# A hybrid decoder layer on one core: the first FFN's residual transposed by VectorE in 32 x 32 blocks, a pair's fourth difference in place, masks and T1 splits bound anew

## The chip, the cores and the metric

The kernel runs on one core of a Trainium2 chip. The metric is the device time of one execution in microseconds (us), the median over several runs; lower is better. A core has five engines with an instruction stream each: TensorE (PE, matrix products and transposes), VectorE (DVE, elementwise work), ScalarE (ACT, activations and copies), GpSimd (POOL, elementwise work and issuing of DMA) and SyncE (SP, issuing of DMA). Each runs its own instructions in order; semaphores join them. Sixteen DMA engines move data between DRAM and the on-chip memory.

## The reference

One decoder layer over 1024 tokens with 16 learned meta tokens ahead of them (T = 1040 rows, D = 1024), all in float32:

```
h = concat(meta, x)
h = h + 1/2 * swiglu(rms_norm(h, g1), ffn1_w_in, ffn1_w_out)     # D_FF = 2816
u = rms_norm(h, g) @ w_in
o = concat[hgrn2(u), stick_breaking(u)]
h = h + o @ w_out
h = h + 1/2 * swiglu(rms_norm(h, g2), ffn2_w_in, ffn2_w_out)
swiglu(h, wi, wo):  g, u = split(h @ wi);  return (silu(g) * u) @ wo
```

What matters here is the first FFN, `h @ ffn1_w_in`, and the residual `h` that is added behind `ffn1_w_out`. The FFN works on transposed activations (features on the partitions, tokens along the free axis), so the residual is wanted transposed too.

## The kernel before

Float32 products are emulated by pairs: a value is split into a rounded high part and the low rest, and a product takes three matmuls (high-high, low-high, high-low). The FFN products use Strassen's scheme in Winograd's form: the two operands are cut into 2 x 2 blocks, and seven products of block sums replace eight. The seven right-hand operands are B11, B21, B22 and T1 to T4. They are built from the normalised tokens for the way in and from the gated activations for the way out.

**The way in** is `fast_in` (L348 to 577), about 11 to 516 us of the span. It goes over 11 pairs of 128-wide blocks of features; the columns of one pair make two `quad`s (L433), the gate's and then the up projection's. A quad makes seven groups of 12 matmuls of 128x512 (`times`, L424; the matmul is L428) in three banks qa, qb and qc. Its weights are loaded by SP (`block`, L371), combined by POOL (`made`, L377 to 382) and split by ACT and DVE (`operand`, L356 to 361: `wh` L358, `wl` L360). The evictions of the gate's quad go through L499 to 506, those of the up's through L508 to 520; L455 and L460 keep the sums u2 and u3 of one bank that others need (the trace names them `u`). PE's group T3 adds onto the bank qb that u2 is read from, so it waits for that.

**The end of a pair** is `combined` (L522 to 540): from the four gated blocks it makes T1, T2, T3 and T4 and stores them to DRAM (`actD`) for the way out. In this first FFN the subtractions run on DVE (`meta` is given). T1, T2 and T4 are tiles `t` (L530) from a ring of two (`t_bufs`, set with the banks in `run`), so T4 needs T1's tile, that is, T1's store has to be done. T3 is made in place in `sg[0,1]`. In the trace the stores of pair q (0 to 10) of the first FFN are called `act1qT<-t` or `act1qT<-sg` (T1 to T4) and `act1qB<-sg` (B11, B21, B22), so `act14T` belongs to its pair 4 and `act19T` to its pair 9; the texts name pairs and the boundaries behind them by this, act14 to act19. Pairs 0 to 3 are the opened ones, whose quads run interleaved.

**The opening** (`open_tokens`, L735 to 902) runs ahead of and within the first quads. It makes the normalised tokens, T2, T3 (`combine` L821, `second` L837) and later T1, T4 and B22 (`later`, L885) while PE already works on the first pairs. Its order on ACT, DVE and SP is written out by hand in `items` (L867). `halve` (L304) splits one block into high (ACT) and low (DVE). The masks that the attention needs much later are cast from float to bytes by one copy on DVE (L864).

**The residual** is transposed beside the pairs by `turn_x` (L950 to 977): 18 places, 9 row blocks of 128 tokens (the last has 16) times 2 halves of the features. For each place SP loads a row block `xrow` of 128x512, PE transposes its four 128x128 squares into a bank (L966, `xt`), ACT copies them to `xts` (L970) and POOL stores them to DRAM (`xD`, L971). `xrow` and `xts` are single buffers. The way out loads `xD` back as `hT` from about 516 us on (`between` in `run`). Beside it goes `split_ahead` (L142 to 178), which splits weights of the later stages ahead of time: SP loads (L152, `early`), ACT and DVE split (L174, L175, `both`), SP stores (L169).

**Order.** PE's order is written by hand: it is the order of the calls. On the other engines the tile framework's scheduler places the instructions by priorities and what they depend on; `issue_after` adds a bound. `open_ev` starts `turn_x` and the splits as steps; `taken`, called after the evictions, advances them in turn.

Of the kernel before, what the change touches and what calls it, by code (L numbers as in the profile page):

```python
# [11 lines left out]
F32 = mybir.dt.float32  # L12
# [8 lines left out]
P = 128  # L21
# [3 lines left out]
META = 16  # L25
T = META + SEQ
# [14 lines left out]
class Block:  # L41
# [262 lines left out]
    def halve(self, pair, src, j):  # L304

        nc = self.nc
        hi, lo = pair
        nc.scalar.copy(hi[:, j, :], src)  # L308
        nc.vector.tensor_sub(lo[:, j, :], src, hi[:, j, :].bitcast(F32))

    def blocks_a(self, hT, gain, c, n, r, ops):

# [35 lines left out]
    def fast_in(self, ops, n, w_in, actD, openers, ev0, open_ev, feed=None, meta=None, spare=None,  # L348
                between=lambda: None, after_opened=lambda: None, late=lambda: None, taken=lambda at, step=True: None):

        nc = self.nc
# [33 lines left out]
        places = [0]  # L385
# [102 lines left out]
        def pair(f, opened=None):  # L488
            sg = {}
            kept = spare(f // 2) if opened and spare else (None, None, None)  # L490

            def tile_of(i, j):
                pool = ev0 if (i, j) == (0, 0) else ev["p"]
                sg[i, j] = kept[2] if (i, j) == (0, 0) and kept[2] is not None else pool.tile(
                    [P, n], F32, tag=f"sg{i}{j}", name="sg", bufs=2 if (i, j) == (0, 0) else 1
                )
                return sg[i, j]

            def gate(i, j, ps, plus):  # L499
                t = tile_of(i, j)  # L500
                if plus is None:
                    at = nc.scalar.activation(t, ps, AF.Silu)
                else:
                    nc.vector.tensor_add(t, ps, plus)
                    at = nc.scalar.activation(t, t, AF.Silu)
                taken(at)

            def up(i, j, ps, plus):  # L508
                t = sg[i, j]
                if plus is None:  # L510
                    at = nc.vector.tensor_mul(t, ps, t)
                else:
                    u = ev["p"].tile([P, n], F32, tag="u", name="u", bufs=2)
                    nc.vector.tensor_add(u, ps, plus)
                    at = nc.vector.tensor_mul(t, u, t)
                taken(at)
                if (i, j) != (0, 1):
                    nc.gpsimd.dma_start(actD[f // 2, f"B{i + 1}{j + 1}"], t)
                else:
                    combined()  # L520

            def combined():  # L522

                sub = (nc.vector if meta else nc.gpsimd).tensor_sub

                def put(name, t):
                    nc.gpsimd.dma_start(actD[f // 2, name], t)

                def made(x, y):
                    t = ev["p"].tile([P, n], F32, tag="t", name="t", bufs=self.t_bufs)  # L530
                    sub(t, x, y)
                    return t

                t1 = made(sg[0, 1], sg[0, 0])
                put("T1", t1)
                t2 = made(sg[1, 1], t1)
                put("T2", t2)
                sub(sg[0, 1], sg[1, 1], sg[0, 1])
                put("T3", sg[0, 1])
                put("T4", made(sg[1, 0], t2))  # L540

            turned = bool(opened) and not feed
            return [
                quad(f * P, gate, opened, 2 * turned, kept[0]),
                quad(D_FF + f * P, up, opened and "second", 1 * turned, kept[1]),
            ]
# [188 lines left out]
    def open_tokens(self, ops, opened, rows_at, ev, operands):  # L735
# [9 lines left out]
        nc, x = self.nc, self.a["x"][0]  # L745
        stt, sub = nc.vector.scalar_tensor_tensor, nc.vector.tensor_sub
# [15 lines left out]
        def apart(name, pool):  # L762
            return [pool.tile([P, 512], F32, name=f"{name}{j}") for j in range(4)]
# [32 lines left out]
        meta = rp.tile([META, D], F32, name="meta")  # L796
# [40 lines left out]
        def second(j):  # L837
            if j == 0:
                rows_at.close()
                pools["masks"].close()  # L840
                operands("T1", "T3", "T2")
            self.halve(ops["T2"], t2[j], j)
            self.halve(ops["T3"], t3[j], j)

        def roots():
            for i, row in enumerate(rb + [meta]):
# [4 lines left out]
        def scales():  # L851
            for i in (2, 3):
                self.row_scale(rb[i], 4 + i)
            self.row_scale(meta, 8)
# [4 lines left out]
                with self.tc.issue_after(at.ins):  # L859
                    self.masks_cut(sd)  # L860

        def combined(j):
            if j == 1:
                nc.vector.tensor_copy(self.masks, sd)  # L864
# [12 lines left out]
        after = {6: turn_b22, 7: turn_b12, 8: turn_meta}  # L877
        for i in range(2, len(order)):
            if i + 2 < len(order):
                next(order[i + 2])  # L880
            items[i]()
            next(order[i])
            after.get(i, lambda: None)()

        def later():  # L885
            for j in range(4):
                self.halve(ops["T1"], b11[j], j)
            yield
            for j in range(4):
                sub(b21[j], b21[j], t2[j])  # L890
# [12 lines left out]

    def meta_in(self, marks):
# [45 lines left out]
    def turn_x(self, pool, xD):  # L950

        nc = self.nc
        places = [(r0, min(P, T - r0), q) for r0 in range(0, T, P) for q in range(2)]

        def load(i):
            r0, m, q = places[i]
            row = pool.tile([P, 512], F32, tag="xrow", name="xrow", bufs=1)
            self.load_rows(nc.sync, row, r0, m, slice(512 * q, 512 * q + 512))
            return row

        row = load(0)
        yield
        for i, (r0, m, q) in enumerate(places):
            ps = self.pin.tile([P, 4, P], F32, tag="qd", name="xt", bufs=2)
            for k in range(4):
                nc.tensor.transpose(  # L966
                    ps[:, k, :m], row[:m, k * P : (k + 1) * P], self.ident[:m, :m]
                )
            t = pool.tile([P, 4, P], F32, tag="xt", name="xts", bufs=1)
            nc.scalar.copy(t[:, :, :m], ps[:, :, :m])  # L970
            nc.gpsimd.dma_start(  # L971
                xD[4 * q : 4 * q + 4, :, r0 : r0 + m].rearrange("k p t -> p k t"),
                t[:, :, :m],
            )
            if i + 1 < len(places):
                row = load(i + 1)
            yield
# [1247 lines left out]
```

## Time and profile before

| | us |
|---|---|
| time, median of 3 runs (2037.3, 2037.41, 2045.62) | 2037.41 |
| the profiled execution's own time | 2047.66 |
| its span in the profile | 2046.0 |
| PE busy (97% of the span) | 1982.2 |
| DVE busy (66%) | 1350.3 |
| ACT busy (42%) | 869.5 |
| POOL busy (29%) | 595.8 |

The profile is of one execution. A line `L428 PE MATMUL qb<-T,wh ...` names the line of the kernel, the engine, the operation, and out<-in by the program's names. A bracket `[4.90 <-DVE u L460]` behind a row of the timeline is the engine's idle time ahead of it and what ended that. "Granted clock" is the share of full clock pulses that PE was given, 1.00 being full.

### The profile page before, as it was taken

What the parts mean: (1) busy time and instruction counts of PE and PEld (TensorE: products, weight loads), DVE (VectorE), ACT (ScalarE), POOL (GpSimd) and SP (SyncE); (2) the same over time, 40 slices, a digit from 0 to 9 for tenths busy, and PEclk for the clock granted to TensorE, in tenths of its full rate; (3) what the DMA queues carried; (4) which work ended last, traced back from release to release, by engine and by line L of the source; (5) the groups of instructions that cost most, each with busy time, mean ns of one, the idle gap of its engine ahead of it and who ended that gap; (6) DMA issues with size and microseconds to landing.
All of it is one profiled execution on the core that took longest, in us unless ns stands there. A gap on an engine that the chain in (4) does not pass through costs nothing.

```text
span 2046.0 us, 30906 instructions
## 1 busy us (share of the span) xinstructions
PE 1982.2 (97%) x11004; PEld 1660.6 (81%) x11004; DVE 1350.3 (66%) x2036; ACT 869.5 (42%) x1758; POOL 595.8 (29%) x708
## 2 busy tenths in 40 slices
PE   7999989999999999999999998999999999999998
PEld 6778777878788888897988887877888888888887
DVE  7966556777686673326767758549476676666774
ACT  6523333443344544446666644435133333334443
POOL 3453333433000002134333332320354454430000
PEclk9999999999999999999999999999999999999999
DMA  7254667655995514543545256673632332369463
GB/s 210 81 177 157 206 218 225 230 204 196 346 316 163 168 48 159 166 139 107 162 117 142 71 187 201 161 251 140 206 117 94 104 112 94 104 236 308 131 198 137
DMA packets 283099, 347.19 MB, mean 170 GB/s; under 512 B 28017, under 2 KB 183153, under 8 KB 282945
## 3 DMA queue, kind: packets, MB, share of 16 engines
q1 hardware_dynamic: 263376, 287.98, 44.3%
q0 software_dynamic: 18528, 57.23, 7.9%
q8 instruction: 87, 1.43, 0.3%
q14 instruction: 68, 0.55, 0.1%
q10 hardware_dynamic: 1040, 0.00, 0.0%
HBM read 233.75 MB, written 111.38 MB: 169 GB/s over the span
## 4 chain that ended last, share of the span: by engine, by line
PE 82%; DVE 6%; DMA 4%; issue 3%; ACT 2%; POOL 2%; SPq 0%; DVEq 0%; POOLq 0%; ACTq 0%
PE o L679 19%; PE qb L428 16%; PE qc L428 11%; PE qa L428 9%; PE proj L249 5%; PE proj L251 5%; PE proj L250 5%; PE flip L1351 2%; PE wo L249 1%; PE wo L250 1%; PE wo L251 1%; PE mq L935 1%; DMA raw<-in_ffn_w_out_dram 1%; PE lvl L1144 1%; PE oacc L1421 1%
## 5 line engine op out<-in xcount | busy, mean ns | idle before, releaser
L428 PE MATMUL qb<-T,wh 128*128 128x512 f32 x1056 | 352.0, 398 | 20.0 <-DVE u L460 18.0
L428 PEld LDWEIGHTS qb<-T,wh 128*128 128x128 f32 x1056 | 201.9, 191 | 69.4 <-issue 20.3
L428 PE MATMUL qa<-B,wh 128*128 128x512 f32 x696 | 228.5, 393 | 1.8 <-ACT T L308 1.8
L249 PE MATMUL proj<-xh,wh 128*128 128x512 f32 (+2 forms) x640 | 216.5, 338 | 0.8 <-DVE st L1044 0.7
L360 DVE TENSOR_TENSOR wl<-s,wh 128x512 fp32r<-128x512 f32 x160 | 179.3, 1121 | 56.5 <-ACT wh L358 54.4
L679 PE MATMUL o<-t,w 128*128 128x512 f32 x924 | 212.9, 391 | 0.2
L679 PE MATMUL o<-parts 128*128 128x512 f32 x924 | 210.2, 389 | 0.6 <-DVE parts L612 0.6
L251 PE MATMUL proj<-xl,wh 128*128 128x512 f32 (+2 forms) x640 | 209.8, 328 | 0.8 <-DVE xl L1806 0.8
L428 PE MATMUL qb<-T,wl 128*128 128x512 f32 x528 | 209.1, 396 | 0.9 <-DVE wl L360 0.9
L250 PE MATMUL proj<-xh,wl 128*128 128x512 f32 (+2 forms) x640 | 209.8, 328 | 0.0
L358 ACT CAST wh<-s 128x512 fp32r<-128x512 f32 x160 | 99.5, 622 | 246.7 <-PE qb L428 189.2
L679 PEld LDWEIGHTS o<-t,w 128*128 128x128 f32 x924 | 172.6, 188 | 37.8 <-issue 0.8
L679 PEld LDWEIGHTS o<-parts 128*128 128x128 f32 x924 | 173.3, 188 | 36.8 <-DVE parts L612 1.0
L382 POOL TENSOR_TENSOR s<-raw 128x512 f32<-128x512 f32 x80 | 110.5, 1381 | 155.1 <-DMA raw<-in_ffn_w_in_dram 92.3
L428 PEld LDWEIGHTS qa<-B,wh 128*128 128x128 f32 x696 | 130.6, 188 | 29.5 <-ACT T L308 2.2
L428 PE MATMUL qa<-B,wl 128*128 128x512 f32 x348 | 135.5, 389 | 0.0
L358 ACT CAST wh<-raw 128x512 fp32r<-128x512 f32 x120 | 74.5, 621 | 139.2 <-PE qc L428 101.0
L251 PEld LDWEIGHTS proj<-xl,wh 128*128 128x128 f32 x640 | 120.5, 188 | 12.2 <-DVE xl L1806 1.2
L249 PEld LDWEIGHTS proj<-xh,wh 128*128 128x128 f32 x640 | 120.7, 189 | 11.4 <-DVE st L1044 1.2
L250 PEld LDWEIGHTS proj<-xh,wl 128*128 128x128 f32 x640 | 120.6, 188 | 9.1
L1503 POOL TENSOR_TENSOR sig<-sig,keep 128x144 f32<-128x144 f32 (+3 forms) x64 | 81.4, 1273 | 134.0 <-DVE keep L1497 82.5
L428 PEld LDWEIGHTS qb<-T,wl 128*128 128x128 f32 x528 | 101.0, 191 | 22.2 <-DVE wl L360 1.8
(390 smaller groups left out, 4084.1 us busy)
## 6 DMA issues: line engine op xcount, KB each, us to landing
raw<-in_ffn_w_in_dram SPq DMA_DIRECT2D x176, 256.0 KB, 3.5
raw<-in_ffn_w_out_dram SPq DMA_DIRECT2D x121, 256.0 KB, 4.4
w2in<-both SPq DMA_DIRECT2D x28, 512.0 KB, 2.9
raw<-in_w_in_dram SPq DMA_DIRECT2D x25, 512.0 KB, 4.1
ks<-kD SPq DMA_DIRECT2D x32, 260.0 KB, 4.8
wout<-both SPq DMA_DIRECT2D x16, 512.0 KB, 4.1
wh<-w2in SPq DMA_DIRECT2D x27, 256.0 KB, 3.6
wl<-w2in SPq DMA_DIRECT2D x27, 256.0 KB, 3.3
```

Of the source, the lines that this page charges most:

```text
L249: nc.tensor.matmul(ps, wh[:, s], xs, start=k == 0, stop=False)
L250: nc.tensor.matmul(ps, wl[:, s], xs, start=False, stop=False)
L251: nc.tensor.matmul(ps, wh[:, s], xl[:, k, c0 : c0 + n], start=False, stop=k == nk - 1)
L358: nc.scalar.copy(hi, src)
L360: nc.vector.tensor_sub(lo, src, hi.bitcast(F32))
L382: taken(op(t, x, y), False)
L428: nc.tensor.matmul(ps, a[:, k, :], b[:, k, :], start=start and k == 0 and i == 0, stop=k == 3 and i == 2, skip_group_check=True,)
L679: nc.tensor.matmul(banks[bank][m], y[:, m * P : (m + 1) * P], z, start=start and at == 0 and e == 0, stop=q == nq - 1 and e == 2, skip_gro ...
L935: nc.tensor.matmul(ps[at : at + 32, :], self.xm[:, 4 * h + k, :], blocks[i, h][:, k, :], start=h == 0 and kk == 0, stop=h == 1 and kk == 1 ...
L1144: nc.tensor.matmul(ps[:, :, c, :], kp[:, P * c : P * c + P], strided(QA, P * c + n, (512 - n, 2), (2 * n, nb), (1, n)), start=True, stop=True,
L1351: self.nc.tensor.transpose(ps[:m, j, :], src[:, s0 : s0 + m], self.ident)
L1503: nc.gpsimd.tensor_mul(sig, sig, keep[:, 1 : nk + 1])
```

## The change

Three things change, all in the first FFN's way in or beside it.

1. **The residual's transposes.** The rows are cut anew: one place with the 16 meta rows and eight of 128 tokens, times two halves. The two meta places go as before (PE, ACT, POOL). In the other 16, DVE transposes the 128x512 tile in 32x32 blocks (`nc.vector.transpose`), each block in its own place, and four SP stores per place, one for each band of 32 partitions, write each block where the whole transpose has it in `xD`. A store moves 64 KB in runs of 32 elements (128 bytes); before, one POOL store moved the place's 256 KB in runs of 512 bytes.
2. **T4 in place.** With `meta` (the first FFN) T4 is made in `sg[1,0]` and stored from there, not in a third `t`.
3. **Bounds in the opening.** `halve` returns its two instructions; the four T1 splits of `later` are issued after the last T3 split on ACT and DVE. The masks copy is moved from the second `combine` to item 7, behind `keep_b22`.

Taking the changed program's order beside the one before: PE loses the 16 groups of four 128x128 transposes, ACT their 16 copies and POOL their 16 stores. DVE gets 16 transposes; in the pairs act14, act15 and act16 they stand in the stretch between the last split of `both` and `u` (L460), in act17 in the up's quad, and none stands in act18 or act19. T4 stands directly behind T3, ahead of `wl` and of the next pair's `u`. The masks copy goes ahead of the opening's first up-gate addition (L511). SP gets 64 stores, each four behind their transpose, with the next `xrow` load behind them.

```diff
         hi, lo = pair
-        nc.scalar.copy(hi[:, j, :], src)
-        nc.vector.tensor_sub(lo[:, j, :], src, hi[:, j, :].bitcast(F32))
+        return (
+            nc.scalar.copy(hi[:, j, :], src),
+            nc.vector.tensor_sub(lo[:, j, :], src, hi[:, j, :].bitcast(F32)),
+        )
...
                 put("T3", sg[0, 1])
-                put("T4", made(sg[1, 0], t2))
+                if meta:
+                    sub(sg[1, 0], sg[1, 0], t2)
+                    put("T4", sg[1, 0])
+                else:
+                    put("T4", made(sg[1, 0], t2))
...
-            self.halve(ops["T3"], t3[j], j)
+            return self.halve(ops["T3"], t3[j], j)
...
-        def combined(j):
-            if j == 1:
-                nc.vector.tensor_copy(self.masks, sd)
-            combine(j)
...
-            7: keep_b22,
+            7: lambda: (keep_b22(), nc.vector.tensor_copy(self.masks, sd)),
         }
...
-        items.update({8 + j: lambda j=j: combined(j) for j in range(4)})
+        items.update({8 + j: lambda j=j: combine(j) for j in range(4)})
...
-            items[i]()
+            last = items[i]()
...
         def later():
-            for j in range(4):
-                self.halve(ops["T1"], b11[j], j)
+            with self.tc.issue_after(last[0].ins), self.tc.issue_after(last[1].ins):
+                for j in range(4):
+                    self.halve(ops["T1"], b11[j], j)
             yield
...
-        places = [(r0, min(P, T - r0), q) for r0 in range(0, T, P) for q in range(2)]
+        places = [(r0, q) for r0 in [0, *range(META, T, P)] for q in range(2)]
...
-        for i, (r0, m, q) in enumerate(places):
-            ps = self.pin.tile([P, 4, P], F32, tag="qd", name="xt", bufs=2)
-            for k in range(4):
-                nc.tensor.transpose(
-                    ps[:, k, :m], row[:m, k * P : (k + 1) * P], self.ident[:m, :m]
+        for i, (r0, q) in enumerate(places):
+            t = pool.tile([P, 512], F32, tag="xt", name="xts", bufs=1)
+            if r0 == 0:
...
+            else:
+                nc.vector.transpose(t, row)
+                dst = xD.rearrange("k p t -> (k p) t")[512 * q : 512 * q + 512]
+                for b in range(4):
+                    nc.sync.dma_start(
+                        dst[:, r0 + 32 * b : r0 + 32 * b + 32].rearrange("(b d) t -> d b t", d=32),
+                        t[32 * b : 32 * b + 32].rearrange("d (b t) -> d b t", t=32),
+                    )
             if i + 1 < len(places):
                 row = load(i + 1)
             yield
```

More of the change, by code (lines that the diff above doesn't have):

```diff
@@ L952, in turn_x @@
         nc = self.nc
-        places = [(r0, min(P, T - r0), q) for r0 in range(0, T, P) for q in range(2)]
+        places = [(r0, q) for r0 in [0, *range(META, T, P)] for q in range(2)]
         def load(i):
-            r0, m, q = places[i]
+            r0, q = places[i]
             row = pool.tile([P, 512], F32, tag="xrow", name="xrow", bufs=1)
-            self.load_rows(nc.sync, row, r0, m, slice(512 * q, 512 * q + 512))
+            cols = slice(512 * q, 512 * q + 512)
+            if r0 == 0:
+                nc.sync.dma_start(row[:META], self.a["meta_tokens"][:, cols])
+            else:
+                nc.sync.dma_start(row, self.a["x"][0][r0 - META : r0 - META + P, cols])
             return row
@@ L962, in turn_x @@
         yield
-        for i, (r0, m, q) in enumerate(places):
-            ps = self.pin.tile([P, 4, P], F32, tag="qd", name="xt", bufs=2)
-            for k in range(4):
-                nc.tensor.transpose(
-                    ps[:, k, :m], row[:m, k * P : (k + 1) * P], self.ident[:m, :m]
-                )
[L969 to L974, printed above, removed]
+        for i, (r0, q) in enumerate(places):
+            t = pool.tile([P, 512], F32, tag="xt", name="xts", bufs=1)
+            if r0 == 0:
+                ps = self.pin.tile([P, 4, META], F32, tag="qd", name="xt", bufs=2)
+                for k in range(4):
+                    nc.tensor.transpose(
+                        ps[:, k, :], row[:META, k * P : (k + 1) * P], self.ident[:META, :META]
+                    )
+                t = t[:, : 4 * META].rearrange("p (k t) -> p k t", k=4)
+                nc.scalar.copy(t, ps)
+                nc.gpsimd.dma_start(
+                    xD[4 * q : 4 * q + 4, :, :META].rearrange("k p t -> p k t"), t
+                )
+            else:
+                nc.vector.transpose(t, row)
[4 more added lines that the diff above has]
+                        t[32 * b : 32 * b + 32].rearrange("d (b t) -> d b t", t=32),
+                    )
             if i + 1 < len(places):
```

## The prediction

> **What bounds the kernel now.** I read the page first: its engine shares and its costliest groups.
>
> ```profile
> span 2046.0 us, 30906 instructions
> PE 1982.2 (97%) x11004; PEld 1660.6 (81%) x11004; DVE 1350.3 (66%) x2036; ACT 869.5 (42%) x1758; POOL 595.8 (29%) x708
> L428 PE MATMUL qb<-T,wh 128*128 128x512 f32 x1056 | 352.0, 398 | 20.0 <-DVE u L460 18.0
> q1 hardware_dynamic: 263376, 287.98, 44.3%
> ```
>
> PE is busy for 97% of the span, so only two things shorten the kernel: fewer instructions on PE, or less of the 64 us in which PE stands still or runs slowly. The third line says that the first FFN's matmuls (L428) stood still 20.0 us, 18.0 of it for the DVE addition `u` of L460. The view of waits says what is ahead of that addition in DVE (columns: total us, times, longest).
>
> ```profile
> PE qb L428 <- DVE u L460: 18.0, 5, 5.2
> DVE t L531 <- DMA act15T<-t: 5.1, 1, 5.1
> DVE t L531 <- DMA act16T<-t: 4.8, 1, 4.8
> DVE t L531 <- DMA act14T<-t: 3.5, 1, 3.5
> DVE t L531 <- DMA act17T<-t: 3.5, 1, 3.5
> POOL xD L971 <- ACT xts L970: 41.2, 13, 5.1
> ```
>
> At the end of pairs act14 to act17, T4 (the third `t` from a ring of two) waits in DVE until T1's store has landed. The PE timeline shows the first matmul after each of the six pair boundaries that PE feels, with PE's idle time ahead of it in brackets, and the one early stall that the change touches (60.00).
>
> ```profile
> 60.00 0.47 PE L428 MATMUL qa<-B,wh 128*128 128x512 f32 x1 [1.80 <-ACT T L308]
> 249.71 0.77 PE L428 MATMUL qb<-T,wh 128*128 128x512 f32 x1 [4.90 <-DVE u L460]
> 299.64 0.77 PE L428 MATMUL qb<-T,wh 128*128 128x512 f32 x1 [5.23 <-DVE u L460]
> 348.44 0.76 PE L428 MATMUL qb<-T,wh 128*128 128x512 f32 x1 [4.99 <-DVE u L460]
> 398.54 0.50 PE L428 MATMUL qc<-T,wl 128*128 128x512 f32 x1 [0.72 <-DVE wl L360]
> 438.87 0.47 PE L428 MATMUL qb<-T,wh 128*128 128x512 f32 x1 [1.93 <-DVE u L460]
> 483.11 0.47 PE L428 MATMUL qb<-T,wh 128*128 128x512 f32 x1 [0.96 <-DVE u L460]
> ```
>
> The chain of waits (start, duration) gives the wait as one of its links and the groups of 12 matmuls behind the gaps.
>
> ```profile
> 215.27 0.44 PE xt L966 x4
> 218.44 2.72 PE qb L428 x12
> 243.14 5.04 DMA act14T<-t
> 249.71 5.46 PE qb L428 x12
> 299.64 4.68 PE qb L428 x12
> 348.44 5.46 PE qb L428 x12
> 438.87 4.57 PE qb L428 x12
> 483.11 3.00 PE qb L428 x12
> ```
>
> Undisturbed, 12 matmuls take 2.72; after a gap of 4.9 they take 5.46, after one of 1.93 they take 4.57: a second price of the gap, paid at half the granted clock. So a boundary costs its gap plus the excess over 2.72: act14 4.90 + 2.74 = 7.64, act15 5.23 + 1.96 = 7.19, act16 4.99 + 2.74 = 7.73, act17 0.72, act18 1.93 + 1.85 = 3.78, act19 0.96 + 0.28 = 1.24. Together 28.3 us.
>
> **The change, part by part.** *T4 in place.* DVE around the first of these boundaries, and T4 of act18:
>
> ```profile
> 244.08 0.68 DVE L360 TENSOR_TENSOR wl<-s,wh 128x512 fp32r<-128x512 f32 x1
> 248.28 0.69 DVE L531 TENSOR_TENSOR t<-sg,t 128x512 f32<-128x512 f32 x1 [3.51 <-DMA act14T<-t]
> 248.88 0.68 DVE L460 TENSOR_TENSOR u<-qb,p 128x512 f32<-128x512 f32 x1
> 440.15 0.68 DVE L531 TENSOR_TENSOR t<-sg,t 128x512 f32<-128x512 f32 x1
> ```
>
> T4 now overwrites `sg[1,0]`, so it needs that tile's own store (B21) landed, not T1's. The DVE waits 3.51, 5.06 and 4.82 (3.5, 5.1, 4.8 above) leave the path. The order of instructions moves too: T4 now stands directly behind T3. In act14 to 16 it was ahead of `u` already; in act17 to 19 it stood behind (440.15, after PE had its `u` at 438.87) and now puts 0.60 (the pitch 248.28 to 248.88) ahead of `u`.
>
> *Transposes on DVE.* Removed from PE: 16 groups of 4, each 0.44 (215.27): 7.0 us on the engine that sets the end. The two 16-row places keep theirs. Removed elsewhere:
>
> ```profile
> L970 ACT COPY xts<-xt x18: 201/579/582, 100.2 to 455.4; 128x512 f32<-128x512 f32 x16, 128x64 f32<-128x64 f32 x2
> L971 POOL DMA_DIRECT2D xD<-xts x18: 760/770/779, 101.0 to 455.9; - x18
> DMA to landing us min/median/max: 2.7/4.8/6.7
> ```
>
> ACT loses 16 x 0.58 = 9.3 us, POOL 16 x 0.77 = 12.3 and part of the 41.2 of waiting; both are busy under half the span, hidden under PE: 0 on the path. Added to DVE: 16 transposes of 128x512. No row shows that operation. Bounds: from below half of a 128x1024 single-input row, 0.35; from above the dearest copy of that size, the masks' 1.71.
>
> ```profile
> 37.09 1.40 DVE L721 TENSOR_SCALAR row<-row,ss_x 128x1024 f32<-128x1024 f32 x2
> 45.45 0.69 DVE L890 TENSOR_TENSOR b<-b,t 128x512 f32<-128x512 f32 x1
> 49.23 1.71 DVE L864 CAST masks<-sd 128x896 uint8<-128x896 f32 x1
> 59.18 0.68 DVE L511 TENSOR_TENSOR sum<-qa,sum 128x512 f32<-128x512 f32 x1
> ```
>
> I take 0.60, the pitch of the 128x512 additions, which have its shape and type. DVE is 66% busy, so most of the 16 hide in its idle time; in act14, 15 and 16 the new order puts one inside the burst ahead of `u`, where it counts. There PE also arrives 0.44 earlier (its transposes are gone), which widens the gap by as much. The gaps become
>
> - act14: 4.90 - 3.51 + 0.60 + 0.44 = 2.43, long enough to drop the clock (1.93 was): + 1.85 = 4.28
> - act15: 5.23 - 5.06 + 1.04 = 1.21; act16: 4.99 - 4.82 + 1.04 = 1.21; I let neither drop it, since 1.21 is nearer to 0.96 (483.11, followed by 3.00) than to 1.93
> - act17: 0.60 + 0.44 = 1.04 (its `wl` is no longer late; between 0 and this)
> - act18: 1.93 + 0.60 + 0.44 = 2.97, + 1.85 = 4.82
> - act19: 0.96 + 0.60 + 0.28 = 1.84
>
> Sum 14.4; gain 28.3 - 14.4 = 13.9. With the transpose at 0.35, 0.75 more; at 1.71, three times 1.1 and two more clock drops (act15, act16): 7.0 less.
>
> [...]
>
> *Stores.* 16 POOL stores of 256 KB become 64 SP stores of 64 KB, the same bytes in runs of 128 B: 32,768 runs. SP now issues per place four stores and, behind them, the next place's `xrow` load; behind these in SP's queue are the raw weight loads (L371) and the loads and stores of the split-ahead (L152, L169), whose consumers are POOL's and ACT's operand work.
>
> ```profile
> 227.38 2.52 SPq L371 DMA_DIRECT2D raw<-in_ffn_w_in_dram  x4
> 256.00:307.00 51.00, 45.77 (x271) 37.22 (x260) 29.27 (x42) 17.98 (x34) 16.99 (x17) 0.93 0.65 220
> 512.00:563.00 51.00, 50.89 (x297) 40.67 (x296) 32.78 (x55) 19.52 (x35) 3.27 (x6) 1.00 0.97 346
> ```
>
> An issue on SP takes 2.52 / 4 = 0.63, so a place costs SP 2.5 us of every 20.9 (L970: 18 starts from 100.2 to 455.4, 355.2 / 17). On the transfer engines the lower bound is nothing (same bytes); the upper takes q1's mean packet, 0.443 x 16 x 2046 / 263,376 = 55 ns: 32,768 x 55 ns / 16 = 113 us over 355, a share of 0.32 more. In the window 256 to 307 (last columns: granted clock, DMA share, GB/s) that lifts 0.65 to 0.97; and 512 to 563 is a stretch with 0.97 where PE still did 50.89 of 51. So I put 0 on the path, hidden by the depth of the raw buffers; without that cover it is the first rival.
>
> [...]
>
> *Masks and T1 splits.* The masks copy (1.71 at 49.23) leaves the stretch ahead of 59.18, and a subtraction of 0.60 pitch (45.45) or its like comes into it: the 1.80 at 60.00 shrinks to 0.7, a gain of 1.1 (between 0 and 1.8).
>
> **Sum.** 13.9 + 7.0 + 1.1 = 22.0. The profiled execution took 2047.66 (span 2046.0 and 1.66 around it): 2025.7 for it. The timed runs were 2037.41, 2037.3 and 2045.62; they scatter by about one boundary's price (7.2 to 7.7), so the median may have met one fewer late T1. If it met all, 2037.4 - 22.0 = 2015.4; if one fewer (7.4), 2022.8. I take the middle, **2019**.
>
> **Rivals.** *1, slower: DVE waits for the small stores.* `xrow` and `xts` are single buffers, so each DVE transpose waits until the four stores before it have landed and the `xrow` load, itself behind them in SP, too. It decides once issue to landing, now 2.7 to 6.7, comes near the 20.9 between places. Everything behind it in DVE (`u`, `wl`) is then late, at act15's price, 7.2 a place; at half the 16 places 58 us: 2019 + 58 = 2077. For it: 4 times as many runs, SP's queue shared with loads. Against: three times the slowest landing is needed.
>
> *2: the DVE burst is the limit anyway*, T4's wait only covered it. For it: act18 stalls 1.93 with no store in the wait. Against: act15 and 16, where 0.17 remains after the wait. All six boundaries at 4.3 cost 25.8, a gain of 2.5; with 7.0 and 1.1, 10.6: 2026.8.
>
> *3: B21's store takes T1's place.*
>
> ```profile
> 239.52 0.54 POOL L518 DMA_DIRECT2D act14B<-sg  x1 [2.15 <-DVE sg L515]
> ```
>
> Issued at 239.52, it lands at 246.2 if it takes the slowest 6.7; T4, ready at 244.08, waits 2.1. Three times that and two clock drops (3.7): 10.0 less, so 2029. Against: the median landing 4.8 is 244.3, some 0.2 late.
>
> [...]
>
> **Chances.** Forecast 0.57, rival 1 0.14, 2 0.17, 3 0.08, 4 0.04. A measurement here can tell about 0.5%: faster is below 2027.2, slower above 2047.6. The forecast and rival 4 are faster but for 0.03; rival 2 lies on the edge (half and half), rival 3 mostly on the near side of no change: faster 0.68, same 0.18, slower 0.14. The range holds all but rival 1 and the far tail: below, all 28.3 plus 7.0 plus 1.8 gone is 2000, which I don't reach, 2005; above, the dear transpose (2026) and rival 3 with some spread, 2036.
>
> **What would show it.** The waits `DVE t L531 <- DMA act..T` gone; PE's idle time ahead of L428 on `u` L460 from 18.0 to about 10; no PE transposes of 128x128; a DVE transpose row near 0.6; PE gap at 60 us under 1. I am wrong if a wait of DVE's transpose or of `xrow` for a DMA shows with several us a place, if PE's gaps at the boundaries stay near 5, or if raw loads become what L428 waits for.

## The result and the profile after

| | before | after |
|---|---|---|
| time, median of 7 runs (us) | 2040.85 (2037.3 to 2046.82) | 2023.35 (2019.63 to 2031.19) |
| the profiled execution's own time | 2047.66 | 2020.56 |
| PE's first matmul of the way out, from the span's start | 516.35 | 490.57 |

The changed kernel is faster: ratio 0.9915, 95% interval 0.9893 to 0.9937, that is 17.3 us (12.9 to 21.8). The two profiled executions lie 27.1 us apart, because the one of before was 6.8 above its kernel's median and the one of after 2.8 below. The third row is the measure used below: the way in begins with the same first matmul in every run (15.4 to 16.5 us), so the start of the way out tells how long it took. Of the 27.1 us, 25.8 came before that point. One execution of the experiment `bounds_alone` below took 3979.15 us instead of some 2041, for which nothing on record gives a reason; its ratio leaves that one out.

The page of after, the same rows as before:

```profile
span 2018.8 us, 30806 instructions
PE 1964.1 (97%) x10940; PEld 1646.2 (82%) x10940; DVE 1356.4 (67%) x2052; ACT 860.8 (43%) x1742; POOL 583.5 (29%) x692
L430 PE MATMUL qb<-T,wh 128*128 128x512 f32 x1056 | 346.0, 391 | 10.1 <-DVE u L462 7.5
q1 hardware_dynamic: 297136, 292.18, 46.0%
```

PE stood still 7.5 us for `u` instead of 18.0, and its matmuls of that group are at 391 ns instead of 398. The view of waits has no T4 waiting for T1's store any more; what DVE's transposes waited for is this, in the whole run:

```profile
DVE xts L983 <- DMA xD<-xts: 3.4, 1, 3.4
DVE xts L983 <- DMA xrow<-in_x_dram: 1.9, 1, 1.9
```

The view of the tile `xts` gives the operation that the profile before did not have, and the landing of the small stores:

```profile
L983 DVE STREAM_TRANSPOSE xts<-xrow x16: 696/701/712, 117.1 to 355.6; 128x512 f32<-128x512 f32 x16
DMA to landing us min/median/max: 1.9/3.1/6.7
```

The PE timeline at the early stall and the six boundaries (start, duration, idle time ahead of it):

```profile
59.87 0.47 PE L430 MATMUL qa<-B,wh 128*128 128x512 f32 x1 [1.94 <-DVE sum L513]
243.06 0.47 PE L430 MATMUL qb<-T,wh 128*128 128x512 f32 x1 [1.47 <-DVE u L462]
286.22 0.47 PE L430 MATMUL qb<-T,wh 128*128 128x512 f32 x1 [2.05 <-DVE u L462]
328.78 0.47 PE L430 MATMUL qb<-T,wh 128*128 128x512 f32 x1 [1.41 <-DVE u L462]
371.37 0.47 PE L430 MATMUL qb<-T,wh 128*128 128x512 f32 x1 [0.95 <-DVE u L462]
414.16 0.47 PE L430 MATMUL qb<-T,wh 128*128 128x512 f32 x1 [1.65 <-DVE u L462]
457.35 0.47 PE L430 MATMUL qb<-T,wh 128*128 128x512 f32 x1 [1.16 <-ACT both L174]
```

And two of the groups behind these gaps in the chain of waits:

```profile
243.06 2.97 PE qb L430 x12
286.22 3.00 PE qb L430 x12
```

None of the six gaps, 8.7 us in sum, dropped the clock: behind 2.05 the twelve matmuls took 3.00, where behind 1.93 they had taken 4.57 before. The early stall is as long as it was (1.80 before, 1.94 now) and has another releaser.

What is late at the boundaries now shows in DVE's timeline at the third of them. DVE works without a pause from 314.51 to 329, and `u` is the last of a queue:

```profile
314.51 1.60 DVE L362 TENSOR_TENSOR wl<-raw,wh 128x512 fp32r<-128x512 f32 x1
316.03 1.77 DVE L517 TENSOR_TENSOR sg<-u,sg 128x512 f32<-128x512 f32 x1
317.73 1.77 DVE L175 TENSOR_TENSOR both<-early,both 128x512 fp32r<-128x512 f32 x1
319.42 0.68 DVE L516 TENSOR_TENSOR u<-qb,p 128x512 f32<-128x512 f32 x1
...
321.83 0.70 DVE L983 STREAM_TRANSPOSE xts<-xrow 128x512 f32<-128x512 f32 x1
...
326.75 0.68 DVE L543 TENSOR_TENSOR sg<-sg,t 128x512 f32<-128x512 f32 x1
327.35 0.69 DVE L362 TENSOR_TENSOR wl<-s,wh 128x512 fp32r<-128x512 f32 x1
327.95 0.68 DVE L462 TENSOR_TENSOR u<-qb,p 128x512 f32<-128x512 f32 x1
```

The change put the transpose (321.83) into that queue. T4 (326.75) stood ahead of `u` at this boundary before, too, but with its wait of 4.82. Three others take 1.60 to 1.77 instead of 0.68; POOL adds beside them:

```profile
314.28 1.28 POOL L384 TENSOR_TENSOR s<-raw 128x512 f32<-128x512 f32 x1 [5.17 <-DMA raw<-in_ffn_w_in_dram]
315.64 1.62 POOL L384 TENSOR_TENSOR s<-s,raw 128x512 f32<-128x512 f32 x1
317.22 1.73 POOL L384 TENSOR_TENSOR s<-raw 128x512 f32<-128x512 f32 x1
```

So the profile of after raises three questions: which part brought the time, whether T4's wait or its place was the price, and whether POOL's additions make the rest.

### The profile page after: what moved, and what is told of

It reads as the page before. It is cut to its first block, busy times and chain, and to the rows that moved or that the text cites. A ratio compares the mean times of both kernels' runs of the same rounds, so it can differ in the third digit from the quotient of the medians.

```text
span 2018.8 us, 30806 instructions
## 1 busy us (share of the span) xinstructions
PE 1964.1 (97%) x10940; PEld 1646.2 (82%) x10940; DVE 1356.4 (67%) x2052; ACT 860.8 (43%) x1742; POOL 583.5 (29%) x692
## 3 DMA queue, kind: packets, MB, share of 16 engines
q8 instruction: 87, 1.43, 0.3%
## 4 chain that ended last, share of the span: by engine, by line
PE 82%; DVE 7%; DMA 5%; issue 3%; ACT 2%; POOL 1%; SPq 0%; DVEq 0%; POOLq 0%; ACTq 0%
PE o L685 18%; PE qb L430 16%; PE qc L430 11%; PE qa L430 10%; PE proj L249 5%; PE proj L251 5%; PE proj L250 5%; PE flip L1366 2%; DMA raw<-in_ffn_w_out_dram 1%; PE wo L250 1%; PE wo L249 1%; PE wo L251 1%; PE mq L937 1%; PE oacc L1436 1%; PE oacc L1438 1%
## 5 line engine op out<-in xcount | busy, mean ns | idle before, releaser
L430 PE MATMUL qb<-T,wh 128*128 128x512 f32 x1056 | 346.0, 391 | 10.1 <-DVE u L462 7.5
L362 DVE TENSOR_TENSOR wl<-s,wh 128x512 fp32r<-128x512 f32 x160 | 183.4, 1147 | 60.4 <-ACT wh L360 59.3
L430 PE MATMUL qc<-T,wh 128*128 128x512 f32 x352 | 118.6, 398 | 0.0
```

The lines of the kernel that those rows point to most:

```text
L362: nc.vector.tensor_sub(lo, src, hi.bitcast(F32))
L430: nc.tensor.matmul(ps, a[:, k, :], b[:, k, :], start=start and k == 0 and i == 0, stop=k == 3 and i == 2, skip_group_check=True,)
```

## The experiments

The twelve were timed in three sets, each beside the kernel before, and a ratio is to the before of its own set. "Way out" is PE's first matmul of it in the one profiled execution, 516.35 in before and 490.57 in after; before's profiled execution was 6.8 above its kernel's median, so a gain read from this column is larger than the one of the medians.

### One part at a time

`t4_alone` has the second part only:

```diff
-                put("T4", made(sg[1, 0], t2))
+                if meta:
+                    sub(sg[1, 0], sg[1, 0], t2)
+                    put("T4", sg[1, 0])
+                else:
+                    put("T4", made(sg[1, 0], t2))
```

> The kernel before with T4 made in place, nothing else. Theory of the prediction (T1's late store is what the boundaries wait for): the four DVE waits of T4 for T1's store vanish, the gaps ahead of the T3 group on L460 fall from 18.0 us to about 6.5 (1.4 at act14, 0.2 at act15 and act16, 1.9 + 0.6 at act18, 1.0 + 0.6 at act19), and of the clock's excess (9.2 us over the six boundaries) 2 to 4 are left: 15 to 19 us faster, ratio 0.991 to 0.993. Rival (DVE's queue is late anyway and the wait only covered it): the gaps stay above 12 us in sum and the ratio is 0.997 or more.

`turn_alone` has the first part only, the new `turn_x`:

```diff
+                nc.vector.transpose(t, row)
...
+                for b in range(4):
+                    nc.sync.dma_start(
...
```

> The kernel before with the residual transposed by DVE and stored by SP, nothing else. Theory of the prediction: 7.0 us of PE's transposes go, and at act14, act15 and act16 T4 still waits for T1's store, with a DVE transpose more in the queue: gaps stay near 5 or grow by up to 1 each. Net 4 to 7 us faster, ratio 0.9965 to 0.998. Rival (the small stores make T1's stores land later and DVE's transpose wait): DVE waits of the transpose for xD or xrow above 10 us in sum, T4's waits above 6 us each, and no gain or a loss, ratio 1.000 or more.

`bounds_alone` has the third part only:

```diff
-            7: keep_b22,
+            7: lambda: (keep_b22(), nc.vector.tensor_copy(self.masks, sd)),
...
+            with self.tc.issue_after(last[0].ins), self.tc.issue_after(last[1].ins):
...
```

> The kernel before with only the moved masks copy and the T1 splits bound behind T3's. Theory of the prediction: the 1.80 us stall near 60 us shrinks to about 0.7, a gain of 1.1 (ratio 0.9995). Rival, from the profile after (1.94 at 59.87, with another releaser): the stall stays between 1.7 and 2.0, no gain at all; what moves is only which operand is late.

| | median us | ratio to before (95%) | way out |
|---|---|---|---|
| t4_alone | 2026.47 | 0.9926 (0.9913 to 0.9939) | 496.32 |
| turn_alone | 2012.88 | 0.9863 (0.9847 to 0.9880) | 482.49 |
| bounds_alone | 2041.96 | 1.0001 (0.9993 to 1.0010) | 515.51 |

The first came as the theory said, with 5.7 us of waiting for `u` left. The third brought nothing: its stall is there, with the releaser that it has in the changed kernel. The masks copy of 1.71 is gone from the stretch ahead of it, but the subtraction that came in its place takes 1.67.

```profile
52.16 1.67 DVE L888 TENSOR_TENSOR b<-b,t 128x512 f32<-128x512 f32 x1
```

```profile
59.97 0.58 PE L430 MATMUL qa<-B,wh 128*128 128x512 f32 x1 [1.99 <-DVE sum L513]
```

The second is the surprise. Both theories expected at most 7 us; the transposes alone bring 28 (0.0137 x 2041.46), more than the whole change. T4 still waits for T1's store there, at 325.42 for 3.06 us, and yet PE hardly stands still:

```profile
321.68 0.68 DVE L460 TENSOR_TENSOR u<-qb,p 128x512 f32<-128x512 f32 x1
325.42 0.69 DVE L531 TENSOR_TENSOR t<-sg,t 128x512 f32<-128x512 f32 x1 [3.06 <-DMA act16T<-t]
```

```profile
PE qb L428 <- DVE u L460: 2.5, 3, 1.4
```

The order on DVE has turned over: `u` stands ahead of T4, so the wait falls where DVE has time. And the transpose of this kernel stands in DVE's natural pause, ahead of the first `u` that waits for the bank qc; it costs nothing there:

```profile
223.50 0.70 DVE L981 STREAM_TRANSPOSE xts<-xrow 128x512 f32<-128x512 f32 x1
226.30 0.69 DVE L514 TENSOR_TENSOR u<-qc,u 128x512 f32<-128x512 f32 x1 [2.09 <-PE qc L428]
```

### Two parts together

`turn_t4` is `turn_alone` with the diff of `t4_alone`; `turn_bounds` is the changed kernel with that diff undone.

> The kernel before with the residual's transposes on DVE and T4 in place, without the third part (masks and T1 splits). Theory (the two parts work against each other through DVE's order: with T4 in place the scheduler puts T4 and, at act14 to act16, the DVE transpose as well ahead of the next pair's addition u, which the transposes alone did not): gaps at the six boundaries as in the changed kernel, 8 to 10 us in sum, ratio 0.990 to 0.992, some 8 to 10 us slower than the transposes alone (0.9863). Rival (it is the masks and T1 splits that cost the changed kernel what the transposes alone had gained): ratio near 0.986.

> The kernel before with the residual's transposes on DVE and with the moved masks copy and bound T1 splits; T4 stays in the ring of t. Theory (T4 in place is the part that costs): DVE's order at the boundaries is that of the transposes alone, gaps under 4 us in sum there, ratio 0.986 to 0.987. Rival (the third part costs): ratio near 0.991.

| | median us | ratio to before (95%) | way out |
|---|---|---|---|
| turn_t4 | 2023.59 | 0.9910 (0.9892 to 0.9927) | 489.23 |
| turn_bounds | 2016.13 | 0.9878 (0.9860 to 0.9897) | 484.28 |

Transposes with T4 in place make the changed kernel's time; without it the time is near that of the transposes alone (the intervals of 0.9878 and 0.9863 overlap). So T4 in place is worth 15 us on the kernel before and costs about 10 beside the transposes: 0.9910 against 0.9863, intervals apart. The third part is at best neutral. In DVE's order by instruction, T4 in place moves both: T4 ahead of `u`, and at act14 to act16 the transpose out of the pause into the queue.

### The place of T4 against its wait

`wait_behind_u` is the kernel before, T4 still in the ring and still waiting, but bound behind the next pair's first `u`:

```diff
...
-                put("T4", made(sg[1, 0], t2))
+                def t4(at=None):
+                    with self.tc.issue_after(at.ins) if at else ExitStack():
+                        put("T4", made(sg[1, 0], t2))
+                t4() if opened or not meta else waiting.append(t4)
...
+                while meta and name == "u2" and waiting:
+                    waiting.pop()(at)
...
```

> The kernel before, with T4 still in the ring of t (so it still waits for T1's store) but bound behind the next pair's first addition u in the pairs that are not opened. Nothing else is changed; PE keeps its transposes. Theory (the price is T4's place ahead of u, not the wait as such): DVE still shows waits of 2 to 5 us of T4 for T1's store at act14 to act17, but the gaps ahead of the T3 group fall from 18.0 us in sum to under 6, and the way in is 20 to 23 us shorter, ratio 0.9895 to 0.992. Rival (the wait itself is the price wherever it stands, since what is behind it in DVE is late then): gaps of 2 us and more at act14 to act17 on other DVE instructions, ratio 0.995 or more.

Ratio 0.9919 (0.9905 to 0.9933), median 2024.61, way out 495.56. The four waits are still there (14.2 us in sum, 16.9 before), and they cost PE little: the way out starts as early as in `t4_alone` (496.32), which has no such wait.

```profile
DVE t L535 <- DMA act16T<-t: 4.1, 1, 4.1
DVE t L535 <- DMA act15T<-t: 3.7, 1, 3.7
DVE t L535 <- DMA act17T<-t: 3.3, 1, 3.3
DVE t L535 <- DMA act14T<-t: 3.1, 1, 3.1
```

```profile
PE qb L429 <- DVE u L461: 3.4, 3, 1.9
```

At act14 to act16 T4 stands one place later in DVE's order, and the order around the six boundaries is otherwise that of before. Moving one subtraction by one place took 20.8 us out of the way in of the profiled execution (16.5 by the medians' ratio), with not a wait removed.

`t4_behind_u` does the same to the changed kernel, T4 in place, the transposes left where they are:

```diff
                 if meta:
-                    sub(sg[1, 0], sg[1, 0], t2)
-                    put("T4", sg[1, 0])
+                    def t4(at=None):
+                        with self.tc.issue_after(at.ins) if at else ExitStack():
+                            sub(sg[1, 0], sg[1, 0], t2)
+                        put("T4", sg[1, 0])
+                    t4() if opened else waiting.append(t4)
...
```

> The changed kernel with T4 (still in place) bound behind the next pair's first addition u in the pairs that are not opened; the DVE transposes stay where the changed kernel has them. Theory (what counts is how many DVE instructions stand ahead of u, not the wait): each of the six gaps falls by 0.6 (1.47, 2.05, 1.41, 0.95, 1.65, 1.16 to about 0.9, 1.4, 0.8, 0.35, 1.05, 0.55), 3 to 4 us faster than the changed kernel, ratio 0.989 to 0.990. Rival (the gaps are set by something else, such as the weights' splits of ACT): gaps within 0.2 of the changed kernel's, ratio 0.991 to 0.992.

Ratio 0.9882 (0.9863 to 0.9901), median 2016.96, way out 486.08. The gaps at act14 to act16 are 0.47, 0.56 and 0.57 (1.47, 2.05, 1.41 in after): they fell by 1.0, 1.5 and 0.8, more than the 0.6 of one instruction. The median is 6 us below the changed kernel's; the intervals of the two ratios overlap at their ends, so the gaps say more than the times here. Why the gaps fell by more than one instruction stays open.

`both_behind_u` binds the transposes behind `u` as well. For that it also moves the call that advances the transposes (`between`) from the end of a quad to the quad's first `u`:

```diff
+                    self.turn_after = at
+                    between()
...
-                nc.vector.transpose(t, row)
+                at = getattr(self, "turn_after", None)
+                with self.tc.issue_after(at.ins) if at else ExitStack():
+                    nc.vector.transpose(t, row)
...
```

> The changed kernel with T4 and the DVE transpose both bound behind the next pair's first addition u (and behind the second quad's) in the pairs that are not opened. Theory (each DVE instruction ahead of u costs its 0.6): against T4 alone bound behind u (gaps 0.47, 0.56, 0.57 at act14 to act16) those three vanish, the way in is some 2 us shorter, about 468 us, ratio 0.9865 to 0.988, the level of the transposes alone. Rival: the transposes now delay the weights' splits behind u, gaps on wl of over 0.5 at many groups, ratio 0.989 or more.

It went the rival's way: ratio 0.9960 (0.9947 to 0.9972), median 2033.21, way out 500.36. PE now waits for the weights' splits, at other groups than before:

```profile
238.53 0.50 PE L431 MATMUL qb<-T,wl 128*128 128x512 f32 x1 [2.15 <-DVE wl L363]
413.77 0.49 PE L431 MATMUL qb<-T,wh 128*128 128x512 f32 x1 [2.85 <-ACT wh L361]
416.56 0.79 PE L431 MATMUL qb<-T,wl 128*128 128x512 f32 x1 [2.29 <-DVE wl L363]
```

The scheduler answered the bound with a different order of DVE over whole pairs; which of its moves made the splits late was not separated.

### DVE slowed by POOL

`sums_dve` is the changed kernel with the four weight sums of a quad on DVE instead of POOL, `turn_sums` the transposes alone with the same:

```diff
+            eng = nc.vector if meta and not opened else nc.gpsimd
-            s1 = made(a21, nc.gpsimd.tensor_add, a22, turns)
+            s1 = made(a21, eng.tensor_add, a22, turns)
...
```

> The changed kernel, with the four weight sums of a quad made by DVE and not by POOL in the seven pairs that are not opened. In the profile after, DVE's 128x512 instructions with two inputs from on-chip memory take 1.7 us instead of 0.68 while POOL adds beside them, and the boundaries' gaps (1.47, 2.05, 1.41, 0.95, 1.65, 1.16) stand behind such a burst. Theory (the residual gaps are that slowdown): with the sums on DVE at 0.60 each the 1.4 to 1.8 us instructions are gone from there, the gaps fall to under 3 us in sum, and it is 5 to 8 us faster than the changed kernel (ratio to before near 0.988). Rival (DVE then waits for the raw weight loads that POOL waits for now, up to 13 us at a time): gaps of 3 us and more with DVE waiting for raw loads, ratio above 0.995.

> The kernel with the transposes alone, with the four weight sums of a quad made by DVE in the pairs that are not opened. Theory (what is left at the boundaries is DVE slowed by POOL's additions): the gap of 1.41 at act18 and the 0.5 ones go, 2 to 4 us faster than the transposes alone, ratio 0.984 to 0.9855. Rival (DVE's waits for raw loads, 17.7 us in sum in the run with the sums on DVE, hold up other DVE work): no faster than the transposes alone, ratio 0.986 or more.

| | median us | ratio to before (95%) | way out |
|---|---|---|---|
| sums_dve | 2019.17 | 0.9885 (0.9872 to 0.9899) | 486.97 |
| turn_sums | 2024.05 | 0.9917 (0.9902 to 0.9931) | 489.84 |

The slowdown is POOL's: between 225 and 480 us the changed kernel has 36 DVE instructions of 128x512 that take over 1.0 us, 28.7 us beyond their 0.68, and both kernels with the sums on DVE have none; the splits `wl` of the sums, after first, then `sums_dve`:

```profile
L362 DVE TENSOR_TENSOR wl<-s,wh 128x512 fp32r<-128x512 f32 x48 | 43.4, 905 | 17.3 <-ACT wh L360 17.2
L362 DVE TENSOR_TENSOR wl<-s,wh 128x512 fp32r<-128x512 f32 x49 | 33.2, 686 | 7.7 <-ACT wh L360 7.5
```

On the changed kernel this brought some 3.6 us in the way in, less than expected; on the transposes alone it lost 7.4. From 200 to 500 us PE stood still 9.6 us in after and 4.4 in `sums_dve`, 3.1 in `turn_alone` and 9.8 in `turn_sums`. So in `sums_dve` most of the boundary gaps did go. How much of that is the faster DVE stays open, since its order changed as well: the transposes of act14 to act16 stand behind `u` there (240.5, 287.1 and 329.2).

The reason that the rival gave is in the waits of both, first `sums_dve`, then `turn_sums`:

```profile
DVE s L384 <- DMA raw<-in_ffn_w_in_dram: 17.7, 9, 3.0
```

```profile
DVE s L382 <- DMA raw<-in_ffn_w_in_dram: 29.9, 12, 4.5
```

Some of them reach PE: in `turn_sums` its gaps of 0.60 at 229.07, 0.62 at 293.12 and 1.24 at 335.47 come behind DVE work that stood behind such a wait. But the largest gaps of both have another cause, T4. In `sums_dve` T4 waits at act17 for B21's store, which is the prediction's third rival, and PE's gap of 1.80 at 365.50 follows, with the granted clock at 0.50 for 3.41 us from 366.24:

```profile
364.15 0.69 DVE L544 TENSOR_TENSOR sg<-sg,t 128x512 f32<-128x512 f32 x1 [2.31 <-DMA act17B<-sg]
```

In `turn_sums` T4 waits for T1's store, at act17 ahead of `u` again and at act18 ahead of a weight sum. PE's gaps of 1.43 at 369.66 and 2.60 at 414.32 follow:

```profile
368.23 0.69 DVE L532 TENSOR_TENSOR t<-sg,t 128x512 f32<-128x512 f32 x1 [3.14 <-DMA act17T<-t]
412.27 0.69 DVE L532 TENSOR_TENSOR t<-sg,t 128x512 f32<-128x512 f32 x1 [1.86 <-DMA act18T<-t]
```

So the two runs show that POOL's additions slow DVE, and not what a DVE free of them would be worth. The slowing is mutual: in after, a DVE subtraction of 128x512 took 0.68 with no POOL addition beside it (326.75) and 1.77 with one (317.73), and POOL's additions took 1.28 with DVE idle (231.88), 1.62 and 1.73 beside DVE (315.64, 317.22). By what means the two hold each other up is not shown.

### The small stores

`wide_stores` is the transposes alone with one store of 256 KB a place in runs of 512 bytes; the blocks stay where DVE left them within their square. `half_runs` cuts each store in two, runs of 64 bytes:

```diff
                 for b in range(4):
-                    nc.sync.dma_start(
-                        dst[:, r0 + 32 * b : r0 + 32 * b + 32]
+                    for c in (0, 16):
+                        nc.sync.dma_start(
+                            dst[:, r0 + 32 * b + c : r0 + 32 * b + c + 16]
...
```

> The kernel with the transposes on DVE alone, but one SP store of 256 KB in runs of 512 bytes for each place instead of four of 64 KB in runs of 128 bytes; this leaves out the putting in place: the 32 x 32 blocks stay where DVE left them within their square. Theory of the prediction (the small stores are hidden): within 0.1% of the transposes alone, 2011 to 2015 us. Rival (small runs load the transfer engines and late raw loads or late T1 stores follow): 4 us or more faster than the transposes alone, the landings of the raw loads shorter than 4.3 us.

> The kernel with the transposes alone, but each store cut into two of 16 tokens: 128 SP stores of 32 KB in runs of 64 bytes, twice the runs and twice the issues, the same bytes. Theory (the stores are hidden with room to spare): landings stay far under the pitch of the places, DVE's transpose waits under 5 us in sum, and the time is that of the transposes alone, ratio 0.985 to 0.9875. Rival (the stores are near the point at which they decide): DVE's transpose waits for xD or xrow above 15 us in sum or raw loads come late, ratio 0.990 or more.

| | median us | ratio to before (95%) | way out |
|---|---|---|---|
| wide_stores | 2020.95 | 0.9899 (0.9881 to 0.9917) | 484.77 |
| half_runs | 2021.40 | 0.9888 (0.9870 to 0.9907) | 489.73 |

Larger runs bring nothing in the way in (484.77 against 482.49). As a clean comparison `wide_stores` failed, though: with fewer stores the scheduler ran all 16 transposes early (113.9 to 197.4 us), and two new gaps of 1.08 and 1.52 came there; it is slower than expected in the rest of the kernel, too, of which the clock is a part: behind the start of the way out its trace has the granted clock at 0.50 for 3.41 us from 556.56 and from 1327.98, that of `turn_alone` only in its last 6 us. With half as large runs the way in took 7.2 us more, and the ratio lies between what the two theories said. But this is one execution, the longest of the five (2023.38; the shortest took 2015.72), and the ratios' intervals of `half_runs` and `turn_alone` overlap (0.9870 to 0.9907, 0.9847 to 0.9880). Part of the 7.2 is the clock: twelve matmuls behind the early stall (2.03 at 60.38) took 4.58, those behind the 1.80 at 59.84 in `turn_alone` 2.98. From 200 to 480 us PE's gaps come to 6.9 us, against 3.1. Late loads do not explain that: DVE's transposes waited 7.3 us in the whole run (4.6 in `turn_alone`), and POOL's sums waited less for raw loads, here from 60 to 500 us `turn_alone`, then `half_runs`:

```profile
POOL s L382 <- DMA raw<-in_ffn_w_in_dram: 68.1, 11, 12.3
```

```profile
POOL s L382 <- DMA raw<-in_ffn_w_in_dram: 44.5, 8, 7.9
```

So the 64 stores are hidden, and whether 128 of half the size cost anything is not shown: the times do not tell it, and what made those gaps larger stays open.

## Why the prediction was right, and where it was not

The direction and the time (2019, range 2005 to 2036) hold against 2023.35. That the total came out so near is luck in part: the forecast added 13.9 for the boundaries and 7.0 for PE's transposes, while T4 alone brings 15, the transposes alone 28 and both together 18. By its steps:

- **T1's late store at the boundaries.** The stall was read rightly, its removal mis-sized: the six boundaries went from 28.3 to 11.2, not to 14.4: 8.7 of gaps, some 0.27 for each of five groups behind them, and 1.16 at act18, where PE stood still another 0.64 for `wl`. These 17.1 and the 7.0 of PE's transposes are 24.1 of the 25.8 that the way in lost. The gaps were near in sum (8.7 against 10.4 predicted) and not one by one (act15 2.05 against 1.21, act18 1.65 against 2.97); the two clock drops at act14 and act18 did not come.
- **What the wait costs.** The prediction took the wait itself as the price. `wait_behind_u` shows that the price was T4's place ahead of `u`: with the same waits behind it the way out starts as early as without them (495.56, 496.32). The prediction saw that the new order puts T4 and the transposes ahead of `u`, 0.60 each, and that was right in order, though T4 moved behind `u` again brought 0.8 to 1.5 a gap (`t4_behind_u`); it did not ask whether the order could be had without it.
- **The transposes.** PE lost its 64 instructions (11004 to 10940), which were priced at 7.0 us, and a piece on DVE costs 0.63 (321.83 to 322.46 in after) against 0.60 forecast. That ACT's and POOL's losses are free was not tested. What was missed is that this part alone turns the scheduler's order round and removes the boundary stalls as well: 28 us. The parts are not additive. 15 for T4 and 28 for the transposes would be 43; together they brought 18, for both work on the same stall and T4 in place undoes the better order.
- **The stores** were hidden, as forecast. The upper bound on the transfer engines, 113 us more of their time, was far off: q1's share went from 44.3% of 2046.0 to 46.0% of 2018.8 us, some 22 more.
- **Masks and T1 splits.** Wrong: 1.1 was forecast, nothing came. The stall stayed at 1.94 and another operand ended it. The term that was mis-sized is the subtraction that takes the copy's place: 0.60 was forecast, in `bounds_alone` it took 1.67 (at 52.16). So DVE's `sum` began at 59.14, hardly earlier than the 59.18 of before. (In `turn_alone`, without this part, that `sum` ends the stall as well: 1.80 at 59.84.)
- **Sum and base.** 22.0 was forecast for the profiled execution, which gained 27.1; the medians moved by 17.5. Taking half of 7.4 off for the medians, 18.4 in all, was of the right kind, since before's profiled execution was 6.8 above its median; that this excess was one late T1 is not shown. Most of the 4.35 by which 2019 is too low is the base: 2037.4 of three runs, 2040.85 of seven. Two readings were loose: the 64 us besides PE's busy time are idle time alone, what PE loses at the lower clock being inside the busy time; and the second rival's 2026.8 goes by 2037.4 where the forecast goes by 2041, so it should be some 2030.

Of the rivals, the second (DVE's queue is the limit anyway) describes what is left at the boundaries, at 0.95 to 2.05 a gap without the clock's price; the third is at most 0.2 us at the boundaries of the changed kernel, at act17 (T4 starts at 369.33 instead of 369.11), while in `sums_dve` it came there with 2.31. The first did not come: the transposes waited 5.3 us in the whole run. The clock held at all six boundaries of the changed kernel, over gaps of up to 2.05; in others of the fourteen profiles it dropped behind gaps of 1.68 and more (last section).

The fastest kernel measured is the transposes alone: 2012.88 us, ratio 0.9863, with the parts two and three of the change left out. It beats the changed kernel (0.9915), the intervals being apart.

## What to carry to other kernels

A wait in an in-order engine costs what stands behind it (`wait_behind_u`: DVE waited 14.2 us with `u` ahead of T4 and PE 3.4 for `u`; before, 16.9 and 18.0): before removing one, look at which instruction the critical engine needs from behind it, and whether moving the waiting instruction by one place is enough. Where a scheduler sets the order, two changes that each help can hurt together, so time each alone and both, and compare the order of the engine that feeds the critical one. Idle time of that engine (here DVE's 2 us pause ahead of the bank qc) is the place for added work; an instruction of the same length in the queue just ahead of a deadline was paid at least in full (T4's 0.6 cost 0.8 to 1.5 a gap).

## What the runs showed of the hardware

How long a gap drops PE's clock is not fixed. The fourteen profiles have 70 PE gaps of 0.9 us and more between 50 and 620 us; the clock dropped where matmuls behind a gap started over 0.3 us apart. Of 29 gaps below 1.68 none dropped the clock, of 35 from 1.68 to 2.85 fourteen did (two of them lie in one drop), and all six of 4.2 and more. Equal gaps differ: 1.93 at 438.87 in before did (4.57 for twelve matmuls), 1.93 in `turn_bounds` did not:

```profile
409.37 0.47 PE L430 MATMUL qb<-T,wh 128*128 128x512 f32 x1 [1.93 <-DVE u L462]
```

```profile
409.37 3.00 PE qb L430 x12
```

In these profiles it went by where the gap lay. From 50 to 620 us all drops of one execution begin on one grid of 3.41 us and last one or two of its cells. In before they begin at 248.65, 296.44, 347.64 and 439.80, which are 14, 15 and 27 cells apart, and last 6.83, 6.83, 6.83 and 3.41, at a granted clock of 0.50. In the fourteen profiles all 18 cells with 1.84 us or more of PE's idle time, outside of a drop, were followed by one, of four with 1.80 to 1.82 one was, and of those with up to 1.77 none. The two gaps of 1.93 show it: the one in before lies within one cell, the one in `turn_bounds` is cut in two by the edge at 408.19. Here are the cell and the next one in before, then the two in `turn_bounds` (the share behind the five engines' times is the granted clock):

```profile
436.38:439.80 3.42, 1.49 (x7) 0.97 (x6) 3.42 (x5) 1.62 (x3) 2.92 (x4) 1.00 0.90 364
439.80:443.21 3.41, 3.41 (x10) 2.67 (x9) 2.83 (x5) 0.00 (x0) 0.55 (x1) 0.50 0.24 97
```

```profile
404.78:408.19 3.41, 2.67 (x12) 1.88 (x10) 3.38 (x7) 1.32 (x3) 1.01 (x2) 1.00 0.66 271
408.19:411.60 3.41, 2.23 (x10) 1.87 (x11) 3.41 (x5) 0.92 (x2) 1.90 (x3) 1.00 0.61 238
```

The grid lay elsewhere from one execution to the next: counted from the span's start in cells of 3.4133 us (92.16 / 27), the drops named here begin 2.89 us into a cell in before (248.65), 1.01 in `sums_dve` (366.24) and 0.19 in `wide_stores` (556.56), and the edge in `turn_bounds` (408.19) lies at 2.00. So for a forecast a gap of about 2 us is a matter of chance; in before the one of 1.93 cost 1.85 us more (4.57 against 2.72). Whether two shorter gaps within one cell add up is not shown. The clock is likely one source of the scatter between executions: the changed kernel's of 2019.63 us had a mean granted clock of 0.999, that of 2031.19 one of 0.995, and by an estimate from these the difference of 0.004 is some 8 of the 11.6 us between them.
